# Forget-gate heads: the inverse sums multiply the outputs of the value products instead of the exponentials

## The chip, the cores and the metric

The kernel runs on one core of a Trainium2 chip. The metric is the device time of one execution in microseconds, from the first to the last instruction and the little that lies around them; the median of several runs is quoted. Five engines work side by side: TensorE (PE in the rows, its weight loads PEld), VectorE (DVE), ScalarE (ACT), GpSimd (POOL) and SyncE (SP), which issues most of the DMAs. Each engine takes its own instructions in the order in which the program lists them, and waits on semaphores for the others.

## What is computed

Two blocks of a network follow each other on 256 tokens of width 1024, two layers each: the first block has two gated feed-forward parts, a mixer with several kinds of attention heads, layer norms and a gated projection; the second block has feed-forward parts, a convolution and a windowed attention, and it carries a second sequence of 256 tokens, the context, beside the first. The change concerns the eight forget-gate heads in the mixer of the first block:

```python
def forgetting_attention(q, k, v, f_logit):
    c = jnp.cumsum(jax.nn.log_sigmoid(f_logit.astype(jnp.float32)), axis=1)
    cT = jnp.transpose(c, (0, 2, 1))
    ...
        s = jnp.einsum('bqhd,bkhd->bhqk', qb, k).astype(jnp.float32) * scale + (cq[..., :, None] - cT[..., None, :])
        p = masked_softmax(s, mask)
        return jnp.einsum('bhqk,bkhd->bqhd', p.astype(v.dtype), v)
```

The mixer concatenates their outputs with those of the other heads and multiplies by `w_out`. The mixer runs in both layers.

## The kernel before

Activations lie with the features on the partitions, as tiles of 128 x 8 x 256 (eight chunks of 128 features, 256 tokens). Almost every weight matrix goes through the same path: a DMA brings a tile of 128 x 1024 into a buffer `r`, ScalarE rounds it into a `w` tile (L496), and VectorE subtracts to get the remainder in a second `w` tile (L502). A product is then three matmuls: high weights by high activations, high by low, low by high. That is `mm3`; one weight tile serves 24 matmuls, and up to three tiles are split ahead of their use.

The program is written as Python generators, called streams. The main stream carries the first sequence through all layers. Filler streams carry the context branch of the second block (tiles `f`, `fh`) and the ada product (tiles `a`, products with `csf`, in groups of four matmuls that the trace counts as eight), which the main stream needs only much later. Before anything is built, a planner runs all streams once against a table of costs and writes down which stream goes next at each step; the build then follows that list. When no main instruction is ready on TensorE by the planner's reckoning, it takes filler; when nothing is ready, it puts in single dummy products (`p<-con 128x128`). So any edit in one stream changes the interleaving of all that follows, though the work in each stream stays the same.

In the mixer two workers take jobs from one list, in this order: two `diff` jobs, two `nsa` jobs, four `fox` jobs (0 to 3). A `fox` job serves two forget-gate heads. Each worker holds two buffers of the slots `k` (`R.wk`, four in all): P for the exponentials, T first for the bias row and then for the transposed exponentials. The steps of a fox job are:

- L511: two rows of bias from the cumulative sums into T.
- the scores: 8 products into two PSUM banks for two heads (16 matmuls in the trace), operands `m` and `k,m_ls`.
- `softmax`: VectorE adds the mask and finds the row maximum (L538), ScalarE takes the exponential and sums it (`k<-p,m_qn`), four pieces in all (128 or 256 columns for each head and each half of the queries); VectorE inverts the four sums in one instruction (L544).
- `scaled`: VectorE multiplies each of the four pieces of P by its inverse sum (L509, `k<-k,m_qs`).
- `transposes`: six TensorE transposes of 128 x 128 through the identity matrix `con` (L593), then ScalarE copies four of them into T (128 x 512) and VectorE two (L523).
- `values`: four products of the values with T into a bank O (eight matmuls `p<-k,m` in the trace).
- `finish`: ScalarE rounds O into chunk 4 + j of the mixer's output (`m<-p`), VectorE writes the remainder (`m<-p,m`), and the flag of that chunk is set.

When all eight flags are set, the products with `w_out` begin; each output chunk of 128 reads the eight input chunks 0 to 7 in order, three matmuls each, so that chunk 7 (the last fox job) is first read after 21 matmuls.

Of the kernel before, what the change touches and what calls it, by code (L numbers as in the profile page):

```python
# [14 lines left out]
OP = mybir.AluOpType  # L15
# [461 lines left out]
class Prog:  # L477
# [699 lines left out]
    def mixer(self, l, xs, acc):  # L1177
        R = self.mr
# [10 lines left out]
        for kc in range(8):  # L1189
# [5 lines left out]
            for tb in range(2):  # L1195
                xh = xs[0][:, kc, tb * 128:tb * 128 + 128]
                xl = xs[1][:, kc, tb * 128:tb * 128 + 128]
                for j, (a, b) in enumerate(((0, 512), (512, 916))):
                    o = ps[tb * 2 + j][:, :b - a]
# [65 lines left out]
        o = VEC["fox_b"][0] + l * 8  # L1265
# [20 lines left out]
        def half(i):  # L1286
            return slice(64 * i, 64 * i + 64)
# [111 lines left out]
        def softmax(P, sm, ng, qk, cost=760.0):  # L1399


            pss = []
            for i in range(2):
                pss.append((yield from R.bank((128, 384))))
            group = []
            for qb in range(2):
                ops = [qk(i, slice(qb * 128, qb * 128 + 128), 128 * (qb + 1)) for i in range(2)]
                for k in range(len(ops[0])):
                    group += [(pss[i][:, seg[qb]], *ops[i][k], k == 0, k == len(ops[0]) - 1) for i in range(2)]
            yield from self.mms(group, cost, 128)  # L1410
            for i, ps in enumerate(pss):
                for qb in range(2):
                    self.masked(ps[:, seg[qb]], self.masks[:, 512 - 128 * qb:640], ng[:, i, qb:qb + 1])
                for qb in range(2):
                    self.act(P[:, i, seg[qb]], ps[:, seg[qb]], AF.Exp, scale=-1.0, bias=ng[:, i, qb:qb + 1],
                             accum_out=sm[:, i, qb:qb + 1])
                R.banks.put(ps)
            self.recip(sm, sm)

        def scaled(P, sm):  # L1420
            for i in range(2):
                for qb in range(2):
                    self.ts(P[:, i, seg[qb]], P[:, i, seg[qb]], sm[:, i, qb:qb + 1], None, OP.mult)

        def transposes(P, T):
            ps = yield from R.bank()
            for i in range(2):
                yield from self.tr(ps[:, i, 0:128], P[:, i, 0:128])
                yield from self.tr(ps[:, i, 128:256], P[:, i, 128:256])
            self.act(T[:, :, 0:256], ps)  # L1430
            R.banks.put(ps)
            ps = yield from R.bank((128, 2, 128))
            for i in range(2):
                yield from self.tr(ps[:, i], P[:, i, 256:384])
            self.cp(T[:, :, 256:384], ps)
            R.banks.put(ps)

        def values(T, O, cols, start=True, stop=True):
            o = (O[0:64], O[64:128])
            yield from self.mms([(o[i], V[:, 0, cols(i):cols(i) + 64], T[:, i, 0:256], start, False) for i in range(2)]  # L1440
                                + [(o[i][:, 128:256], V[:, 1, cols(i):cols(i) + 64], T[:, i, 256:384], False, stop)
                                   for i in range(2)], 710.0)

        def finish(src, c):
            OH, OL = out
            self.act(OH[:, c], src)
            self.tt(OL[:, c], src, OH.bitcast(F32)[:, c], OP.subtract)
            self.flags.add(f"{fl_}o{c}")
# [25 lines left out]
        def fox(w, j):  # L1474
            yield from self.until(f"{fl_}fox{j // 2}")
            yield from self.until(fl_ + "pre")
            sm, ng = w.small
            T = yield from self.take(R.wk, (128, 2, 384))
            RT = T[:, 0, 0:256]
            for i in range(2):  # L1480
                b, k = half(i), 2 * j + i
                self.ts(RT[b], cT[b], fm[b, 2 + k:3 + k], fm[b, 10 + k:11 + k], OP.mult, OP.add)

            def qk(i, q, n):
                b = half(i)
                return [(PB[b, j, q], PB[b, 4 + j, :n]), (late[0][b, q], RT[b, :n])]

            P = yield from self.take(R.wk, (128, 2, 384))
            yield from softmax(P, sm, ng, qk, 1420.0)
            scaled(P, sm)  # L1490
            yield from transposes(P, T)
            R.wk.put(P)
            yield from self.until(fl_ + "out")
            O = yield from R.bank((128, 256))
            yield from values(T, O, lambda i: fv + (2 * j + i) * 64)
            R.wk.put(T)
            finish(O, 4 + j)
            R.banks.put(O)

        def diff(w, j):  # L1500
            yield from self.until(fl_ + "diff")
# [44 lines left out]

        out = []
        jobs = [(diff, 0), (diff, 1), (nsa, 0), (nsa, 1), (fox, 0), (fox, 1), (fox, 2), (fox, 3)]

        def worker(w):  # L1550
# [586 lines left out]
```

## Time and profile before

| | us |
|---|---|
| median of 3 runs | 2863.72 |
| lowest and highest of them | 2862.18, 2868.28 |
| the profiled execution, whole | 2864.28 |
| its span, first to last instruction | 2862.5 |
| busy in it: TensorE, weight loads | 2815.1, 2672.2 |
| busy in it: VectorE, ScalarE | 1929.5, 1403.4 |

The mean granted clock of TensorE is 0.992 of full speed. All times in the rows come from the profiled execution. "Busy" of TensorE counts from a matmul's start to its modelled end, and matmuls overlap, so a stretch can be busy and still have lost time between starts; the step from one start to the next is what a matmul takes in a row of them. A step of time in brackets behind a row is the time for which the engine was idle before it, with the one that released it.

### The profile page before, as it was taken

The numbers are of one execution on the slowest core, as the hardware profiler recorded it, in microseconds if no ns is written. First come the engines' busy times: TensorE is split into PE (matmuls) and PEld (weight loads), VectorE is DVE, ScalarE is ACT, GpSimd is POOL, SyncE is SP. The second block draws the span as 40 slices with busy tenths as digits, with TensorE's granted clock in tenths as the row PEclk, the third lists the DMA queues.
The fourth block names the chain that finished last, engine by engine and source line by source line (L and its number), as shares of the span: only waits on it lengthen the run. The fifth ranks groups of instructions, "written<-read, shape, count | busy, mean of one in ns | idle before, by whom it ended". The sixth has DMA issues, their size and how long they took to land.

```text
span 2862.5 us, 55997 instructions
## 1 busy us (share of the span) xinstructions
PE 2815.1 (98%) x23348; PEld 2672.2 (93%) x23348; DVE 1929.5 (67%) x3332; ACT 1403.4 (49%) x2200; POOL 0.2 (0%) x4
## 2 busy tenths in 40 slices
PE   8999999999999999899999999999999999999998
PEld 7999888999999788699899999989999999987998
DVE  4556676656755677899776569998755655576645
ACT  4545544544644554444565454455544554555543
POOL 0000000000000000000000000000000000000000
PEclk9999999999999999999999999999999999999999
DMA  9754554555555664655565555565655565653453
GB/s 342 268 191 164 203 206 170 173 189 188 200 190 186 231 236 141 223 190 183 193 221 184 192 170 198 184 214 166 214 193 184 173 206 186 207 188 134 156 190 113
DMA packets 152846, 553.93 MB, mean 194 GB/s; under 512 B 16272, under 2 KB 26256, under 8 KB 152464
## 3 DMA queue, kind: packets, MB, share of 16 engines
q1 hardware_dynamic: 151728, 548.30, 56.1%
q8 instruction: 183, 3.00, 0.4%
q10 hardware_dynamic: 864, 2.05, 0.2%
q14 instruction: 71, 0.58, 0.1%
HBM read 549.24 MB, written 1.05 MB: 192 GB/s over the span
## 4 chain that ended last, share of the span: by engine, by line
PE 86%; DVE 8%; ACT 3%; DMA 2%; issue 1%; SPq 0%; DVEq 0%; ACTq 0%
PE p L574 84%; DVE w L502 2%; ACT k L496 1%; PE p L593 1%; DVE m L517 1%; DMA a<-ada_w 1%; ACT w L496 1%; DVE f L517 1%; DMA r<-W 1%; DVE m L502 1%; DVE p L538 0%; DVE k L509 0%; ACT m L496 0%; ACT f L496 0%; DVE f L502 0%
## 5 line engine op out<-in xcount | busy, mean ns | idle before, releaser
L574 PE MATMUL p<-m,w 128*128 128x256 f32 x10896 | 1389.7, 282 | 8.7 <-ACT w L496 6.0
L574 PEld LDWEIGHTS p<-m,w 128*128 128x128 f32 x10896 | 1330.0, 189 | 32.9 <-issue 18.1
L502 DVE TENSOR_TENSOR w<-r,w 128x1024 fp32r<-128x1024 f32 (+1 forms) x884 | 1056.2, 1214 | 448.5 <-ACT w L496 438.5
L496 ACT ACTIVATE w<-r 128x1024 fp32r<-128x1024 f32 (+1 forms) x884 | 899.9, 1045 | 438.5 <-PE p L574 289.9
L574 PE MATMUL p<-k,w 128*128 128x256 f32 x4192 | 539.6, 282 | 0.6 <-ACT k L496 0.5
L574 PEld LDWEIGHTS p<-k,w 128*128 128x128 f32 x4192 | 514.0, 188 | 6.8 <-issue 5.6
L574 PE MATMUL p<-f,w 128*128 128x256 f32 x3600 | 492.7, 284 | 1.3 <-ACT k L496 0.9
L574 PEld LDWEIGHTS p<-f,w 128*128 128x128 f32 x3600 | 451.3, 189 | 20.4 <-issue 10.5
L496 ACT ACTIVATE k<-p 128x256 f32<-128x256 f32 (+1 forms) x200 | 80.6, 403 | 354.0 <-PE p L574 351.5
L574 PE MATMUL p<-fh,w 128*128 128x256 f32 x1776 | 252.8, 285 | 0.0
L574 PEld LDWEIGHTS p<-fh,w 128*128 128x128 f32 x1776 | 229.0, 189 | 4.8 <-issue 2.8
L502 DVE TENSOR_TENSOR k<-k,p 128x256 f32<-128x256 f32 x176 | 73.5, 418 | 171.2 <-ACT k L496 170.9
L496 ACT ACTIVATE k<-k 128x256 fp32r<-128x256 f32 (+1 forms) x180 | 74.8, 418 | 123.1 <-DVE k L502 123.1
L502 DVE TENSOR_TENSOR k<-k,k 128x256 fp32r<-128x256 f32 (+1 forms) x176 | 74.8, 425 | 85.2 <-ACT k L496 85.2
L496 ACT ACTIVATE m<-m 128x512 f32<-128x512 f32 (+4 forms) x123 | 64.9, 546 | 92.2 <-DVE m L502 55.7
L517 DVE SCALAR_TENSOR_TENSOR m<-m,vec,m 128x241 f32<-128x241 f32 (+14 forms) x240 | 100.0, 471 | 0.0
L517 DVE SCALAR_TENSOR_TENSOR f<-fh,vec,f 128x241 f32<-128x241 f32 (+14 forms) x240 | 99.2, 470 | 0.0
L574 PE MATMUL p<-a,csf 128*32 128x384 f32 x768 | 86.3, 530 | 3.7 <-DMA a<-ada_w 3.2
L496 ACT ACTIVATE k<-p,m_qn 128x128 f32<-128x128 f32 x96 | 39.0, 419 | 55.5 <-DVE m_qn L538 53.0
L496 ACT ACTIVATE fh<-f_sq 128x256 fp32r<-128x256 f32 x66 | 27.6, 418 | 76.8 <-DVE f_sq L502 61.3
L496 ACT ACTIVATE f_sq<-p 128x256 f32<-128x256 f32 x66 | 24.9, 378 | 71.6 <-PE p L574 71.6
L538 DVE CUSTOM_DVE_ANT_0 p<-p,masksb 128x128 f32<-128x128 f32 (+2 forms) x128 | 55.1, 456 | 4.6 <-PE p L574 3.0
(234 smaller groups left out, 1414.4 us busy)
## 6 DMA issues: line engine op xcount, KB each, us to landing
r<-W SPq DMA_DIRECT2D x876, 512.0 KB, 4.2
a<-ada_w SPq DMA_DIRECT2D x96, 768.0 KB, 4.9
a<-phi_k SPq DMA_DIRECT2D x8, 512.0 KB, 3.5
a<-phi_v SPq DMA_DIRECT2D x8, 512.0 KB, 3.7
m<-xT SPq DMA_DIRECT2D x4, 256.0 KB, 4.2
r<-W SPq DMA_DIRECT2D x8, 128.0 KB, 4.0
f<-ctxT ACTq DMA_DIRECT2D x1, 1024.0 KB, 13.6
out<-m SPq DMA_DIRECT2D x4, 256.0 KB, 2.5
```

The source lines that it names most:

```text
L496: self.nc.scalar.activation(out, in_, func, **kw)
L502: self.nc.vector.tensor_tensor(out=out, in0=a, in1=b, op=op)
L517: self.nc.vector.scalar_tensor_tensor(out, a, s, b, op0=op0, op1=op1)
L538: self.nc.vector.tensor_tensor_reduce(ps, ps, mask, -1.0, 3e38, OP.add, OP.min, ng)
L574: self.nc.tensor.matmul(out, l, r, start=start, stop=stop, skip_group_check=True)
L593: self.nc.tensor.transpose(out, in_, ident[:k, :k])
```

## The change

In a fox job the exponentials in P are no longer multiplied by the inverse sums before they are transposed. Instead VectorE spreads the four inverse sums of the job over a tile of 128 queries x 128 features for each half of the queries (in P's first 256 columns, once the transposes have read them), TensorE transposes the two halves into a PSUM bank `pm`, so that they lie with the features on the partitions as the outputs do, ScalarE copies the output bank O into T, and VectorE multiplies the copy by `pm`. `finish` then reads T in place of O. P, T and one more bank are held until then. The diff and nsa heads keep their scaling.

```diff
             P = yield from self.take(R.wk, (128, 2, 384))
             yield from softmax(P, sm, ng, qk, 1420.0)
-            scaled(P, sm)
             yield from transposes(P, T)
-            R.wk.put(P)
+
+            rb = P[:, 0, 0:256]
+            self.cp(rb.rearrange("p (q a f) -> p q a f", q=2, a=2),
+                    sm.rearrange("p a (q o) -> p q a o", o=1).to_broadcast([128, 2, 2, 64]))
             yield from self.until(fl_ + "out")
             O = yield from R.bank((128, 256))
             yield from values(T, O, lambda i: fv + (2 * j + i) * 64)
-            R.wk.put(T)
-            finish(O, 4 + j)
+            pm = yield from R.bank((128, 256))
+            for qb in range(2):
+                yield from self.tr(pm[:, qb * 128:qb * 128 + 128], P[:, 0, qb * 128:qb * 128 + 128])
+            o = T[:, 0, 0:256]
+            self.act(o, O)
             R.banks.put(O)
+            self.tt(o, o, pm, OP.mult)
+            R.banks.put(pm)
+            R.wk.put(P)
+            finish(o, 4 + j)
+            R.wk.put(T)
```

The planner's list differs from the first mixer on. Over the whole program TensorE gets 16 transposes and 9 dummy products more, VectorE 32 scalings less, 8 copies and 8 products more, ScalarE 8 copies more; everything else is there as often as before.

TensorE at the end of layer 1's mixer, from the transposes of the last two jobs (P in `k_170` and `k_172`) to the first `w_out` product (`m_34`, `w_687`). Before (`a_65` and `a_66` are ada tiles, `f_row` an ada row, `k_169` and `k_171` the jobs' T):

```order
L593 MATMUL p_329_13144<-con,k_170_13089 128x128 x4
L593 MATMUL p_332_13179<-con,k_170_13089 128x128 x2
L593 MATMUL p_331_13173<-con,f_row_13171 128x128 x2
L593 MATMUL p_330_13166<-con,k_172_13114 128x128
L593 MATMUL p_331_13173<-con,f_row_13171 128x128
L593 MATMUL p_330_13166<-con,k_172_13114 128x128
L574 MATMUL p_334_13191<-a_65_13121,csf 32x384 x4
L574 MATMUL p_333_13183<-k_169_13086,m_31_11295 64x256 x2
L574 MATMUL p_333_13183<-k_169_13086,m_31_11295 64x128 x2
L593 MATMUL p_330_13166<-con,k_172_13114 128x128 x2
L593 MATMUL p_335_13212<-con,k_172_13114 128x128 x2
L574 MATMUL p_334_13191<-a_66_13192,csf 32x384 x4
```

and of the changed kernel a piece of the same stretch (`f_6` and `f_7` are the context's activations, `p_336` a bank of its projection, `p_343` the bank `pm` of the first of the two jobs):

```order
L574 MATMUL p_336_13073<-f_6_11156,w_686_12859 128x256
L593 MATMUL p_338_13118<-con,k_172_13054 128x128
L574 MATMUL p_336_13073<-f_6_11156,w_685_12858 128x256
L574 MATMUL p_336_13073<-f_7_11157,w_685_12858 128x256
L574 MATMUL p_336_13073<-f_6_11156,w_686_12859 128x256
L593 MATMUL p_338_13118<-con,k_172_13054 128x128
L593 MATMUL p_341_13174<-con,k_172_13054 128x128 x2
L574 MATMUL p_340_13147<-k_169_13034,m_31_11330 64x256 x2
L574 MATMUL p_340_13147<-k_169_13034,m_31_11330 64x128 x2
L593 MATMUL p_343_13184<-con,k_170_13037 128x128 x2
```

The ada groups have left this stretch, products of the context's projection stand between the transposes (48 of them from the last score block to `w_out`), and two transposes into `pm` follow each job's value products.

ScalarE at the same place, from the last exponential to the first weight split behind the mixer (`m_34` is the rounded output). Before:

```order
L496 ACTIVATE f_row_13171<-p_241_11250 128x384
L496 ACTIVATE k_169_13086<-p_329_13144 128x2x256
L496 ACTIVATE m_34_12432<-p_333_13183 128x256
L496 ACTIVATE k_171_13111<-p_330_13166 128x2x256
L496 ACTIVATE m_34_12432<-p_336_13216 128x256
L496 ACTIVATE w_695_13234<-r_348_13050 128x1024
```

and of the changed kernel:

```order
L496 ACTIVATE k_169_13034<-p_337_13097 128x2x256
L496 ACTIVATE w_693_13151<-r_347_13078 128x1024
L496 ACTIVATE k_171_13051<-p_338_13118 128x2x256
L496 ACTIVATE k_169_13034<-p_340_13147 128x256
L496 ACTIVATE m_34_12362<-k_169_13034 128x256
L496 ACTIVATE f_sq_13203<-p_336_13073,hb_126 128x256
L496 ACTIVATE k_171_13051<-p_342_13179 128x256
L496 ACTIVATE m_34_12362<-k_171_13051 128x256
L496 ACTIVATE w_695_13225<-r_348_13155 128x1024
```

Each job has one evacuation more, from the output bank into T, ahead of the rounding; a weight split and an activation of the context branch stand between them.

## Rows read from the trace of the kernel before

**Rows 1.** The page: TensorE's busy time, and the chain that ended last.
```profile
PE 2815.1 (98%) x23348; PEld 2672.2 (93%) x23348; DVE 1929.5 (67%) x3332; ACT 1403.4 (49%) x2200; POOL 0.2 (0%) x4
...
PE 86%; DVE 8%; ACT 3%; DMA 2%; issue 1%; SPq 0%; DVEq 0%; ACTq 0%
```

**Rows 2.** Busy time by stretches: from:to, length, then the columns named first.
```profile
core 0: us, PE busy (x) PEld busy (x) DVE busy (x) ACT busy (x) POOL busy (x), PEclk, DMA share, GB/s
...
456.00:469.80 13.80, 13.60 (x117) 11.35 (x116) 11.18 (x27) 7.27 (x16) 0.00 (x0) 1.00 0.67 248
1129.10:1147.40 18.30, 17.95 (x157) 14.62 (x156) 14.51 (x45) 8.67 (x26) 0.00 (x0) 1.00 0.29 113
1147.40:1163.30 15.90, 12.11 (x91) 6.54 (x87) 9.28 (x39) 5.28 (x20) 0.00 (x0) 0.79 0.45 149
```

**Rows 3.** Timeline, end of layer 0's mixer: start, length, engine, line, what.
```profile
464.14 4.91 PE L574 MATMUL p<-fh,w 128*128 128x256 f32 x39
...
469.78 9.85 PE L574 MATMUL p<-m,w 128*128 128x256 f32 x81
```

**Rows 4.** Timeline, end of layer 1's mixer.
```profile
1147.43 0.49 PE L574 MATMUL p<-m 64*128 64x128 f32 x4
...
1150.25 0.85 PE L574 MATMUL p<-a,csf 128*32 128x384 f32 x8
...
1152.03 1.01 DVE L509 TENSOR_SCALAR k<-k,m_qs 128x128 f32<-128x128 f32 x4
...
1152.46 1.18 PE L593 MATMUL p<-con,k 128*128 128x128 f32 x6 [1.36 <-DVE k L509]
...
1156.07 0.69 PE L593 MATMUL p<-con,f_row 128*128 128x128 f32 x2 [2.43 <-ACT f_row L496]
...
1163.32 8.85 PEld L574 LDWEIGHTS p<-m,w 128*128 128x128 f32 x75 [0.17 <-issue]
```

**Rows 5.** Timeline: five transposes' loads, a block of value products, an ada group.
```profile
443.52 0.57 PEld L593 LDWEIGHTS p<-con,k 128*128 128x128 f32 x5
...
1145.85 0.87 PE L574 MATMUL p<-k,m 128*64 128x256 f32 x8
...
1146.65 0.16 PEld L574 LDWEIGHTS p<-a,csf 128*32 128x32 f32 x8 [0.17 <-issue]
```

**Rows 6.** Groups by line and shape: count | busy us, mean ns | idle before.
```profile
L496 ACT ACTIVATE w<-r 128x1024 fp32r<-128x1024 f32 x876 | 897.1, 1051 | 438.5 <-PE p L574 289.9 <-DMA r<-W 96.2 <-issue 33.7
...
L502 DVE TENSOR_TENSOR k<-k,p 128x256 f32<-128x256 f32 x176 | 73.5, 418 | 171.2 <-ACT k L496 170.9
...
L496 ACT ACTIVATE k<-p 128x256 f32<-128x256 f32 x176 | 67.0, 381 | 353.6 <-PE p L574 351.5 <-issue 1.7
...
L509 DVE TENSOR_SCALAR k<-k,m_qs 128x256 f32<-128x256 f32 x40 | 13.9, 347 | 0.0
...
L496 ACT ACTIVATE k<-p 128x512 f32<-128x512 f32 x20 | 12.1, 603 | 0.4 <-PE p L593 0.2
...
L509 DVE TENSOR_SCALAR k<-k,m_qs 128x128 f32<-128x128 f32 x40 | 11.3, 283 | 0.7
```

**Rows 7.** The spreading copy of the diff heads: count, ns least/median/most.
```profile
L523 DVE COPY k<-m_nr x4: 293/293/295, 386.6 to 1095.9; 128x256 f32<-128x256 f32 x4
```

**Rows 8.** Timeline of covered jobs: a transpose's wait, and a row of exponentials.
```profile
443.13 0.30 PE L593 MATMUL p<-con,k 128*128 128x128 f32 x1 [0.40 <-DVE k L509]
...
1138.66 0.37 ACT L496 ACTIVATE k<-p,m_qn 128x128 f32<-128x128 f32 x1 [2.14 <-DVE m_qn L538]
...
1139.46 0.37 ACT L496 ACTIVATE k<-p,m_qn 128x128 f32<-128x128 f32 x1
```

**Rows 9.** The chain that ended last, in order of time: start, length, what.
```profile
1153.92 1.72 ACT k L496 x8
```

**Rows 10.** Timeline, the layer norm behind mixer 1.
```profile
1196.80 0.85 PE L574 MATMUL p<-a,csf 128*32 128x384 f32 x8 [1.77 <-DMA a<-ada_w]
...
1198.77 1.05 PE L574 MATMUL p<-con,m 128*128 128x2 f32 x8 [1.11 <-DVE m L517]
```

More of the change, by code (lines that the diff above doesn't have):

```diff
@@ L1495, in fox @@
             yield from values(T, O, lambda i: fv + (2 * j + i) * 64)
+            pm = yield from R.bank((128, 256))
[3 more added lines that the diff above has]
+            self.act(o, O)
+            R.banks.put(O)
+            self.tt(o, o, pm, OP.mult)
+            R.banks.put(pm)
+            R.wk.put(P)
+            finish(o, 4 + j)
             R.wk.put(T)
-            finish(O, 4 + j)
-            R.banks.put(O)
         def diff(w, j):
```

## Prediction

> **What bounds the kernel now.** I read the page first: TensorE is busy for 98% of the span and carries 86% of the chain that ended last [rows 1]. So an instruction taken off another engine is worth only the TensorE time that was lost in waiting for it, and a TensorE instruction that is added costs its own length unless it falls into such a lost stretch. The question is where TensorE loses time near the forget-gate jobs. There are eight of them, four in each mixer; each serves two heads.
>
> The second view is a table by stretches [rows 2]. 456.0:469.8 ends the mixer of layer 0, 1147.4:1163.3 that of layer 1. Both hold the last forget-gate jobs, up to the first product with w_out. In layer 0 the array is busy for 13.60 of 13.8 us at a granted clock of 1.00, in layer 1 for 12.11 of 15.9 us at a mean granted clock of 0.79. The third view, the timeline, says why. In layer 0 the last transposes are followed by 39 products of the filler (the context branch, which runs where the main stream waits) [rows 3]. In layer 1 the filler has run out of ready products before the last two score blocks; from there on only three groups of the ada product stand between main instructions. So TensorE waits 1.36 us for VectorE's scaled exponentials of one job and 2.43 us for a row of ScalarE, and after these pauses part of the stretch runs at the lower clock level, 1.2 GHz [rows 2, 4].
>
> How much is lost there? From the first score product at 1147.43 to the first w_out product at 1163.32 it is 15.9 us [rows 4]. The work in it at full-clock prices: two score blocks, 1147.43 to 1150.25, 2.8 us [rows 4]; 15 transposes at 0.57 / 5 = 0.114 us, 1.7; two blocks of value products at 0.80 (the step from 1145.85 to 1146.65), 1.6; three ada groups at 0.78 (the step from 1146.65 to 1147.43), 2.3 [rows 4, 5]. Sum 8.4, lost 7.5 us. The same account for layer 0, 456.02 to 469.78: one score block 1.4, six transposes 0.7, two value blocks 1.6, one ada group 0.8, and 69 filler products (the last 39 in [rows 3]) at 8.85 / 75 = 0.118 us a product with its weights [rows 4], 8.1. Sum 12.6 of 13.8, lost 1.2. For the covered pair before, 1129.1:1147.4 in layer 1, it leaves 1.6 of 18.3. So a covered pair of jobs loses about 1.4 us, the uncovered one 7.5.
>
> **The change, part by part.** *Removed:* four scalings a job on VectorE, 2 x 0.347 + 2 x 0.283 = 1.26 us [rows 6], 10.1 us in all. They stood between the last exponential and the transposes. TensorE waited for them for up to 0.40 us in a covered job [rows 8] and for 1.36 us in the uncovered one [rows 4]. Off the path they are worth nothing: VectorE is busy for 11.18 of 13.8 us in the covered end [rows 2].
>
> *Added on TensorE:* two transposes a job, 16 x 0.114 = 1.8 us [rows 5], on the engine that sets the end. *Added on VectorE:* a copy that spreads the inverse sums, 0.293 (the like copy in the diff heads) [rows 7], and a product with a PSUM operand, 0.418 [rows 6]; 5.7 us in all, less than what went. *Added on ScalarE:* an evacuation of 0.381 us a job [rows 6], 3.0 us in all, on an engine that is busy for 7.27 of 13.8 us [rows 2]. The evacuation and the product lie one behind the other on the way from the value products to the finished rows: 0.8 us and two handovers. Nobody waits for that in the first seven jobs of a kernel; in the last job of a layer w_out begins with the chunks 0 to 6, 21 x 0.118 = 2.5 us, before it first reads chunk 7. Were that cover gone, it would cost about 0.8 us a layer.
>
> *A new wait on ScalarE:* the rounding of the finished rows waits for VectorE's product, and behind it in ScalarE's order stand the next evacuation and a weight split. It holds them for about 0.4 us and a handover. A split serves 24 matmuls (24 x 0.118 = 2.8 us) and three tiles are split ahead, so I put it at nothing.
>
> *Moved:* the order is planned anew. Both programs hold 5,640 filler products and 384 ada matmuls, so no work is won by it, only idle time. In the new order 48 filler products stand between the last score blocks and w_out of layer 1, where the old one had the three ada groups. Is TensorE then the last there? Its work is 2.8 + 16 x 0.114 + 1.6 + 48 x 0.118 = 11.9 us, plus the 1.4 that a covered pair loses: 13.3. The chain beside it: the second job's exponentials end at 1155.64 [rows 9], 1.0 us sooner when the first job's scalings (1152.03, [rows 4]) no longer stand ahead of its masks, so 1154.6; then two evacuations at 0.603, a weight split at 1.05 [rows 6], value products 0.8, two transposes 0.2 and some handovers, estimated at 1159 to 1159.5, or 12 us after 1147.43. TensorE is the later by a little, so the end is covered. It becomes 2.6 us shorter and holds 5.7 - 2.3 - 0.3 = 3.1 us more filler (0.3 for three transposes of ada rows that left), which is missing elsewhere: 5.7 us, or 6.1 with its four new transposes counted in their own term, the same as 7.5 - 1.4.
>
> The ends of this term are nothing (the pause returns elsewhere, [rows 10]) and 7.5 us (nothing lost at all). I take 6.1, as the covered pairs of both layers agree. Of the other six jobs I expect no gain: most of what they lose is change between shapes, not waiting. Each transpose now waits for its own exponential, where it waited for a scaling; the nearest waits are 0.40 us in a covered job [rows 8] and 1.36 [rows 4], so the difference lies between -0.4 and about 1 us a job. I take 0, since one wait of a kind replaces another, and keep the ends for the range.
>
> The sum: -6.1 + 1.8 = **-4.3 us**. The profiled execution took 2864.28 us (its span of 2862.5 and 1.8 around it), 0.6 above the median 2863.72. So 2860.0 for that execution and 2859.4, say **2859.5**, for the median.
>
> One reading beside this: by busy time the end of layer 1 has 3.8 us free; by weight loads it is loaded for 6.54 of 15.9 us, against 11.35 of 13.8 in layer 0 [rows 2]. The Trainium skill (Perfetto Trace Analysis, Identifying the Most-Contended Engine) holds matmul busy time a poor measure, because matmuls are pipelined, and judges by the share of weight loads. At layer 0's share the stretch would take 6.54 / 0.82 = 8.0 us, 7.9 less, and the kernel 2863.7 - 7.9 + 1.8 = 2857.6, an estimate by that page's rule; by busy time it would be 2861.7. I follow neither; the time by the rule lies in the part of the first rival and moves no chance, since an ada group shows 0.16 us of loads [rows 5] and holds the array for 0.78.
>
> **The rivals.** (1) *More comes back.* The covered jobs, too, lose less, because no transpose waits for VectorE. For it: such waits are in the trace [rows 8]. Price: 0.4 us in six jobs and the whole 7.5 in the tail, -2.4 - 7.5 + 1.8 = -8.1, 2855.6. It counts as faster from -5.7, 2858.0. (2) *The pause only moves.* The filler spent in the tail is missing where TensorE waited next, in the layer norm after mixer 1, which already shows waits of 1.77 and 1.11 us [rows 10]. For it: the convolution taps that the context branch needs next begin later on VectorE. Against: the ada groups pushed out of the tail can fill just such waits. Price: the 16 transposes stay, 2863.7 + 1.8 = 2865.5. (3) *Slower by a new wait.* TensorE takes its row in order, and the transposes now stand behind one exponential each, with three filler products, 0.35 us, between them. If TensorE waits out a job's whole row of exponentials, 1.72 us [rows 9], it loses 8 x 1.72 = 13.8 us and the sum is +9.5, 2873.2; it decides from 1.25 us a job on (8 x 1.25 = 4.3 + 5.7). Against it: the exponentials follow each other at 0.40 us (two in 0.80, [rows 8]), hardly slower than the fillers between.
>
> **How the numbers follow.** A measurement of this kernel can tell 0.2%, 5.7 us, from no change. Chances: forecast, 2858 to 2863, 0.50; rival 1, below 2858, 0.28; rival 2, 2863 to 2869.4, 0.14; rival 3, above, 0.08. So faster 0.28, same 0.64, slower 0.08. The range for 8 in 10 goes from 2855.5 (rival 1 whole) to 2866.5 (rival 2 with 1 us of rival 3).
>
> **What would show it.** Right: in the changed kernel's end of mixer 1 filler stands between the transposes, no TensorE wait there is over 0.5 us, the granted clock is 1.00, and it is about 13.3 us from the second last score block to w_out. Wrong: that stretch is still near 15.9 us; transposes wait over 1 us a job for exponentials; or the layer norm behind it has a pause of several us that was not there.

## The result and the profile after

The changed kernel takes **2882.87 us** (median of 4 runs, 2882.14 to 2885.80); the kernel before took 2864.26 beside it (4 runs). The ratio is 1.0062 with a 95% interval of 1.0050 to 1.0075: slower by 18.6 us. The forecast was 2859.5, its range ended at 2866.5.

The page of the changed kernel, first the busy time, then the chain that ended last by engine, as in [rows 1]:

```profile
PE 2823.5 (98%) x23382; PEld 2682.3 (93%) x23382; DVE 1929.3 (67%) x3316; ACT 1408.2 (49%) x2208; POOL 0.2 (0%) x4
PE 77%; DVE 14%; ACT 4%; DMA 2%; issue 2%; SPq 0%; DVEq 0%; ACTq 0%
```

TensorE is still busy for 98%, but it carries 77% of the chain in place of 86%, and VectorE 14% in place of 8%. So TensorE waits longer, and above all for VectorE. The busy share hides it: the span is 17.8 us longer and the busy time 8.4, because matmuls at half clock, and the 34 records of them that were added, are busy too.

The place on which the forecast rested did what was forecast. The end of mixer 1, from the second last score block to `w_out`, in a table by stretches (columns as in [rows 2]):

```profile
1155.40:1169.00 13.60, 13.04 (x114) 10.82 (x113) 9.51 (x32) 8.05 (x26) 0.00 (x0) 1.00 0.17 53
```

The same stretch in the timeline of TensorE, as [rows 4] show it of before:

```profile
1155.39 0.49 PE L574 MATMUL p<-m 64*128 64x128 f32 x4
...
1158.96 1.33 PE L574 MATMUL p<-f,w 128*128 128x256 f32 x9
1160.71 0.33 PE L593 MATMUL p<-con,k 128*128 128x128 f32 x1 [0.42 <-ACT k L496]
1160.80 0.60 PE L574 MATMUL p<-f,w 128*128 128x256 f32 x3
1161.24 0.27 PE L593 MATMUL p<-con,k 128*128 128x128 f32 x1
...
1167.98 0.87 PE L574 MATMUL p<-k,m 128*64 128x256 f32 x8
1168.78 0.44 PE L593 MATMUL p<-con,k 128*128 128x128 f32 x2
1168.98 1.19 PE L574 MATMUL p<-m,w 128*128 128x256 f32 x8
```

Filler stands between the transposes, the longest wait is 0.42 us, the granted clock is 1.00, and the stretch has become 13.6 us (forecast 13.3; before 15.9, at 0.79 of the clock).

The loss lies elsewhere. The two programs were laid over each other by the 10,896 matmuls `p<-m,w` of the main stream, which stand in the same sequence in both. The table gives, for five stretches of the main stream (times of the kernel before) in one profiled execution of each kernel, what the steps from one matmul to the next hold above the usual step of their kind: as pauses (a step over 0.3 us too long) and as half clock (the other steps in stretches with a granted clock of 0.5).

| stretch, us | pauses before, after | half clock before, after | longer by |
|---|---|---|---|
| up to the layer norm ahead of mixer 1, 0 to 959 | 18.9, 21.8 | 3.7, 2.2 | 2.0 |
| that layer norm and mixer 1, 959 to 1163 | 18.6, 20.8 | 1.9, 5.4 | 3.6 |
| layer norm behind it, to 1229 | 8.0, 8.2 | 0.6, 2.2 | 2.2 |
| convolution, 1381 to 1506 | 7.6, 9.9 | 3.7, 6.8 | 7.9 |
| the rest | 21.5, 21.6 | 1.8, 1.3 | 2.1 |
| sum | 74.6, 82.3 | 11.7, 17.9 | 17.8 |

Of the 17.8 us, 7.7 are pauses, 6.2 half clock and 3.9 all else, the 16 transposes and 9 dummy products that were added among it. How they divide depends on what is taken as the usual step: other choices (by the shape of the matmul alone, or of the next one) give 2 to 9 us of pauses and 5 to 7 of half clock. The runs bear the half clock out: the mean granted clock is 0.989 to 0.991 in the four runs of the changed kernel, and 0.992 in the mean of 20 runs of the kernel before. ("Longer by" counts filler done earlier or later too. By 1012 us the changed kernel is 3.9 us late, but has 18 filler products more behind it. By the first `w_out` product of layer 1 it has done 3 transposes of ada rows and 24 records of ada products less and is 5.7 us late; at 0.114 and 0.10 us each that is some 8.4 us behind.)

Two of its pauses stand before the last forget-gate jobs. The timeline of VectorE and TensorE at the first, where the rotary embedding waits:

```profile
1035.21 0.70 PE L574 MATMUL p<-m,w 128*128 128x256 f32 x3
1035.45 3.50 DVE L502 TENSOR_TENSOR w<-r,w 128x1024 fp32r<-128x1024 f32 x3
1038.87 0.69 DVE L523 COPY m<-p 128x512 f32<-128x512 f32 x1
1039.61 1.38 PE L574 MATMUL p<-m,con 128*128 128x256 f32 x4 [3.70 <-DVE m L523]
1040.42 4.33 PE L574 MATMUL p<-m,w 128*128 128x256 f32 x21
```

TensorE waits 3.70 us for a copy of 0.69 us, in front of which three weight remainders stand in VectorE's order. Not all of this is new. The kernel before waits 3.14 us near this place, for a memset of VectorE, in its timeline of TensorE:

```profile
1030.64 0.63 PE L574 MATMUL p<-a,m_PTc 128*16 128x256 f32 x8 [3.14 <-DVE p L550]
1031.20 2.74 PE L574 MATMUL p<-m,w 128*128 128x256 f32 x21
```

New are 0.6 us of waiting and the 21 products behind it, which take 4.33 us in place of 2.74. The second pause is new as a whole: from 1080 to 1130 us the kernel before has no wait over 0.23 us. In the timeline of all three engines there, one weight remainder stands ahead of the masks of an `nsa` job, and the masks ahead of the exponentials:

```profile
1112.57 1.23 DVE L502 TENSOR_TENSOR w<-r,w 128x1024 fp32r<-128x1024 f32 x1 [0.52 <-ACT w L496]
1113.07 0.44 PE L593 MATMUL p<-con,k 128*128 128x128 f32 x2 [0.47 <-ACT m_PTc L496]
1113.72 0.29 DVE L538 CUSTOM_DVE_ANT_0 p<-p,masksb 128x128 f32<-128x128 f32 x1
1114.69 0.37 ACT L496 ACTIVATE k<-p,m_qn 128x128 f32<-128x128 f32 x1 [1.67 <-DVE m_qn L538]
1115.65 2.29 PE L574 MATMUL p<-f,w 128*128 128x256 f32 x9 [2.14 <-ACT k L496]
```

Behind it TensorE works at the lower level, 1.2 GHz, and so it does in the convolution (where the kernel before has two such stretches of 6.8 us). The two longest in the table by stretches:

```profile
1115.60:1125.80 10.20, 10.15 (x44) 7.55 (x46) 5.33 (x12) 4.58 (x11) 0.00 (x0) 0.51 0.44 177
1419.40:1429.60 10.20, 10.20 (x51) 8.68 (x50) 6.22 (x17) 6.99 (x14) 0.00 (x0) 0.51 0.46 155
```

None of this is in a forget-gate job. So two theories stand against each other. **Theory 1:** the planner's new order costs the time; the new job itself costs its transposes and little more. **Theory 2** (rival 3 of the prediction, widened): the job's own new instructions and waits cost it.

### The profile page after: what moved, and what is told of

Same layout as the page of the kernel before. It is cut to its first block, busy times and chain, and to the rows that moved or that the text cites. A ratio compares the mean times of both kernels' runs of the same rounds, so it can differ in the third digit from the quotient of the medians.

```text
span 2880.3 us, 56086 instructions
## 1 busy us (share of the span) xinstructions
PE 2823.5 (98%) x23382; PEld 2682.3 (93%) x23382; DVE 1929.3 (67%) x3316; ACT 1408.2 (49%) x2208; POOL 0.2 (0%) x4
## 4 chain that ended last, share of the span: by engine, by line
PE 77%; DVE 14%; ACT 4%; DMA 2%; issue 2%; SPq 0%; DVEq 0%; ACTq 0%
PE p L574 76%; DVE w L502 5%; DVE f L517 3%; DVE m L517 2%; ACT k L496 2%; PE p L593 1%; DMA r<-W 1%; ACT w L496 1%; DMA a<-ada_w 1%; DVE m L502 1%; DVE k L502 1%; DVE p L538 1%; ACT f L496 0%; ACT m L496 0%; ACT f_sq L496 0%
## 5 line engine op out<-in xcount | busy, mean ns | idle before, releaser
L502 DVE TENSOR_TENSOR k<-k,k 128x256 fp32r<-128x256 f32 (+1 forms) x176 | 74.8, 425 | 85.2 <-ACT k L496 85.2
```

The source lines that it names most:

```text
L502: self.nc.vector.tensor_tensor(out=out, in0=a, in1=b, op=op)
```

## Experiments: job and order apart

The planner and the build run the same generators, so the planner can be shown one job while the build emits the other into the same steps. That gives the two missing corners of a square.

**New job in the old order.** `pm` is the second half of O's bank, so that no step is added. Against the changed kernel the edit is in pieces:

```diff
+            if self.planning:
+                scaled(P, sm)
+                yield from transposes(P, T)
...
+            else:
...
-            O = yield from R.bank((128, 256))
+                OB = yield from R.bank()
+                O, pm = OB[:, 0], OB[:, 1]
...
-            pm = yield from R.bank((128, 256))
...
-                yield from self.tr(pm[:, qb * 128:qb * 128 + 128], P[:, 0, qb * 128:qb * 128 + 128])
+                    self.nc.tensor.transpose(pm[:, qb * 128:qb * 128 + 128], P[:, 0, qb * 128:qb * 128 + 128], self.con_("ident"))
```

> The planner is shown the old fox job, the build puts the new one into the same places: every filler product, ada group and dummy product stands where it stood in the kernel before, and each job's two transposes into pm follow its value products directly. Theory 1 (the new order of the filler costs the time, the new job itself only its 16 transposes and short waits, 0.95 us a layer as mixer 0 of the changed kernel showed): 2864.3 + 1.9 = about 2866 us; the stretch from 1083 to 1229 us no longer than before by more than 1 us, the one from 1380 to 1506 the same as before. Theory 2 (the new job's own instructions and waits cost it, above all in mixer 1): about 2880 us, with mixer 1 longer by 7 to 8 us. It decides between them at 2873.

Measured: ratio 1.0017 (1.0008 to 1.0026), 4.9 us over the kernel before. **Old job in the new order** is the converse: the planner sees the new job, the build emits the scaled exponentials and leaves the two steps of the transposes empty.

```diff
+            if self.planning:
...
+            else:
+                scaled(P, sm)
...
+                pm = yield from R.bank((128, 256))
+                for qb in range(2):
+                    yield 0.0
+                finish(O, 4 + j)
```

> The converse: the planner is shown the new job, the build emits the old one (scaled exponentials, no transposes into pm, no evacuation ahead of the product) with the filler where the changed kernel has it. Theory 1: the pauses before the forget-gate jobs of mixer 1 and in the convolution stretch stay, so 2882.9 - 1.9 = about 2881 us. Theory 2: about 2864 us, as before. It decides between them at 2873.

Measured: ratio 1.0076 (1.0064 to 1.0089), 21.8 us over the kernel before.

| | old order | new order |
|---|---|---|
| old job | 1 | 1.0076 |
| new job | 1.0017 | 1.0062 |

With either job the new order costs 13 to 22 us. The job costs 4.9 us in the old order (2.3 to 7.5), more than the 1.9 that theory 1 gave it, though far from the 16 of theory 2; in the new order it looks 4 us cheaper than the old one, but there the intervals overlap. Theory 2 falls. The traces show the same: the old job in the new order has the pause of the changed kernel at its place, with the same three remainders ahead of the same copy,

```profile
1036.78 3.50 DVE L502 TENSOR_TENSOR w<-r,w 128x1024 fp32r<-128x1024 f32 x3
1040.19 0.68 DVE L523 COPY m<-p 128x512 f32<-128x512 f32 x1
1040.93 2.07 PE L574 MATMUL p<-m,con 128*128 128x256 f32 x4 [4.53 <-DVE m L523]
```

and the new job in the old order has the pauses of the kernel before in its end of mixer 1 [rows 4], though nothing is scaled there any more (the transposes of the inverse sums are those of L1511):

```profile
1150.38 0.49 PE L574 MATMUL p<-m 64*128 64x128 f32 x4
...
1155.50 1.26 PE L593 MATMUL p<-con,k 128*128 128x128 f32 x6
1159.39 0.69 PE L593 MATMUL p<-con,f_row 128*128 128x128 f32 x2 [2.63 <-ACT f_row L496]
...
1166.98 0.44 PE L1511 MATMUL p<-con,k 128*128 128x128 f32 x2
1167.17 1.06 PE L574 MATMUL p<-m,w 128*128 128x256 f32 x7
```

Its stretch is 16.8 us (1150.38 to 1167.17), no shorter than the 15.9 of before. So the 2.3 us won in the end of mixer 1 were won by filler placed there, not by the scalings that left.

**The new job in one layer alone**, planned as such; for layer 0 the edit is

```diff
+            if l == 0:
+                yield from transposes(P, T)
...
+            else:
+                scaled(P, sm)
...
```

and for layer 1 the same with `if l == 1:`.

> The new job in layer 0 alone, planned as such; layer 1 keeps the old job. Theory 1 in its simple form (the loss in mixer 1 comes from planning the new job there): 2864.3 + 0.95 = about 2865 us. If it is the filler that layer 0 displaces (21 products fewer are done by its w_out) that is missing in mixer 1, then the pauses of 3.98 us at 1035 and 2.4 us at 1113 of the changed kernel are here too and it takes 2872 us or more. Theory 2: half of the loss, about 2873 us.

> The new job in layer 1 alone; layer 0 and all that is planned up to mixer 1 are those of the kernel before. Theory 1 in its simple form: all of the loss but layer 0's part, about 2881 us. If the displaced filler of layer 0 starts it, then 2864.3 + 0.95 = about 2865 us or a little less. Theory 2: about 2873 us.

Measured: 1.0056 (1.0043 to 1.0068), 16 us, for layer 0 alone; 1.0023 (1.0014 to 1.0032), 6.6 us, for layer 1 alone. The simple form of theory 1 falls: most of the loss comes with the edit in layer 0, though nothing is edited behind that layer. In the timeline of TensorE of the kernel with layer 0 alone both pauses of above stand in mixer 1, at the same instructions, where that kernel runs the old job:

```profile
1035.92 1.64 PE L574 MATMUL p<-m,con 128*128 128x256 f32 x4 [2.96 <-DVE m L523]
...
1111.99 2.29 PE L574 MATMUL p<-f,w 128*128 128x256 f32 x9 [2.14 <-ACT k L496]
```

The first is no longer than the 3.14 us of the kernel before, and the loss is not that of the changed kernel over again. Laid over the kernel before by the same products, the profiled execution with layer 0 alone is 6.3 us late at 2500 us and 13.2 at 2619 (its span is 13.2 us longer); the changed kernel goes from 16.2 to 16.6 there. So about half of its loss arises in the second block, far behind any forget-gate job.

Nor is it filler missing after layer 0: it is 21 products behind at `w_out` of layer 0, but at 544 us and still at 900 both programs have done the same filler and ada products, product for product, and go apart only after that. What carries over is then the planner's reckoning of its clocks and of the filler's credit; that is concluded from the counts, no run took it apart.

## Experiments: is it this order, or any other?

**The kernel before with one number of the planner changed**, and no instruction of the streams added, removed or altered:

```diff
-FILLS = (0.25, 0.35, 0.025, 0.0, 0.01, 0.126, 0.056, 0.05, 0, 0.11, 0.35, 1.12, 0.08, 0.25, 0.05, 0.07, 0, 0.1)
+FILLS = (0.25, 0.35, 0.026, 0.0, 0.01, 0.126, 0.056, 0.05, 0, 0.11, 0.35, 1.12, 0.08, 0.25, 0.05, 0.07, 0, 0.1)
```

The third share is that of the mixer of layer 0. In the second kernel the seventh, that of the mixer of layer 1, is 0.058 in place of 0.056.

> The kernel before with one number of the planner changed: the share of filler in the mixer of layer 0 is 0.026 in place of 0.025. No instruction is added, removed or altered, only the order of the filler differs from mixer 0 on. Theory 1a (the old order was a chosen one, and nearly any other costs 10 us or more, whatever the job looks like): 2874 us or more against 2866.3. Theory 1b (only the new job makes the planner find a bad order): 2866 us, within 3.

> The same for the mixer of layer 1: 0.058 in place of 0.056, so the order differs from mixer 1 on alone. Theory 1a: slower too, but by less, since only the second half of what can go wrong is drawn anew: 2869 to 2876 us. Theory 1b: 2866 us, within 3.

Measured: 1.0055 (1.0042 to 1.0068), 15.8 us, and 1.0021 (1.0012 to 1.0029), 6.0 us. That is the size of the change in layer 0 and in layer 1 alone, 16 and 6.6, with the job untouched. Both lie where theory 1a put them. Two draws do not show that nearly any order costs so much, and one thing beside the order did differ: the planner put in 19 and 7 of its own dummy products more (38 and 14 records `p<-con`). At 0.23 us each (32 records in 3.73 us, below) they are worth at most 4.4 and 1.6 us. The trace of the first shows two long pauses in mixer 1, behind VectorE and ScalarE:

```profile
1041.26 1.06 PE L574 MATMUL p<-a,m_PTc 128*16 128x256 f32 x8 [3.89 <-DVE p L550]
...
1120.57 2.72 PE L574 MATMUL p<-f,w 128*128 128x256 f32 x11 [4.19 <-ACT k L496]
```

The first stands at the instruction at which the kernel before waits 3.14 us, the second is new. Its pauses sum up to 85.2 us in place of 74.6, by the account of the table above, and here too 7.9 us of the loss arise between 2500 and 2619 us.

**Both kernels with the planner's shares chosen anew**, in the same way for both, by the planner's own reckoning. For the changed kernel:

```diff
+FILLS = (0.25, 0.3704, 0.0261, 0, 0.0059, 0.1393, 0.0447, 0.0514, 0, 0.0679, 0.346, 1.12, 0.08, 0.2578, 0.0769, 0.07, 0.0058, 0.1003)
```

and for the kernel before:

```diff
+FILLS = (0.25, 0.35, 0.0258, 0.0057, 0.0093, 0.1152, 0.0421, 0.0447, 0, 0.0735, 0.35, 1.12, 0.08, 0.25, 0.0574, 0.07, 0, 0.1)
```

> The changed kernel with the planner's 18 shares chosen anew for it (13 of them differ by a few per cent to a quarter, the other code is the same), as those of the kernel before had been chosen for the old job. Theory 1a: the loss of order goes, and what is left is the job's own cost in place, 4.5 us as e1 measured: 2866 to 2871 us on a chip where the kernel before takes 2866. Theory 1b: it stays at 2880 or above.

> The kernel before with its shares chosen anew in the same way and with as many trials. It gives what the old job takes at its best order by the same search, so that the two jobs are compared with both orders chosen for them: 2862 to 2868 us expected by both theories, 1 to 5 us under e7_after_retuned if the new job costs what e1 measured.

Measured: 1.0002 (0.9993 to 1.0011) for the changed kernel, 1.0006 (0.9996 to 1.0016) for the kernel before. (12 shares differ in the changed kernel, one of them up from 0 and the others by 0.3% to 54%, where the expectation says 13 and at most a quarter.) The 18.6 us of the change are gone, by numbers that touch only the order and the planner's own dummy products (9 fewer than in the changed kernel, as many as in the kernel before). The pauses in its profiled execution are 75.1 us and its half clock 11.9, about those of the kernel before. One execution is not the kernel, though: the profiled one of the old job with new shares has the lowest granted clock of its 11 runs (0.990; the others 0.991 to 0.993), and its span is 6.7 us over that of the kernel before, where the ratio is 1.0006. With an order chosen for each, the two jobs cost the same, within about 0.1%.

## Experiments: the clock behind the pauses

If the half clock follows pauses, dummy products in the pauses should save it. A table tells the build before which TensorE instruction how many go in; the order is untouched:

```diff
+        n = BUSY.get(self.issued, 0)
...
+        if n and banks.free:
+            ps, ident = banks.get((128, 128)), self.con_("ident")
+            for _ in range(n):
+                self.nc.tensor.matmul(ps, ident, ident, start=True, stop=True, skip_group_check=True)
+            banks.put(ps)
...
```

> The kernel before, its order untouched, with dummy products (identity by identity, 89 in 15 places) put into the pauses of TensorE over 0.9 us from 300 us on, as many as fit into each pause at 0.23 us a dummy product. Theory 2a (the half-clock stretches follow pauses in which the array is idle; busy with dummies it stays at full clock): of the 11.7 us that the half clock costs in the profiled run of before nearly all comes back, 2866.5 - 10 = about 2856 us. Theory 2b (dummies do not hold the clock, or the pauses themselves are the whole price): 2866.5 us, within 3.

> The changed kernel, its order untouched, with 109 dummy products in 20 pauses in the same way. It tells how much of the loss of the new order is the half clock behind the pauses (17.8 us in its profiled run, 6.1 more than in before) and how much the pauses. Theory 2a: 2884 - 15 = about 2869 us. Theory 2b: 2884 us, within 3.

> The changed kernel with the shares chosen anew (e7_after_retuned) and dummy products in 14 of its pauses. Theory 2a: 2868 - 10 = about 2858 us, a version that is faster than both kernels. Theory 2b: 2868 us, within 3.

(In the changed kernel one of the 20 places found no free bank, so 102 dummies in 19 pauses went in.) Measured against the kernel before: 1.0038 (1.0024 to 1.0052), 1.0141 (1.0127 to 1.0155) and 1.0075 (1.0063 to 1.0088), all three slower than without dummies (1, 1.0062 and 1.0002). Both theories missed, because many of the dummies waited themselves. In the changed kernel at the pause of the rotary embedding:

```profile
1044.28 0.70 PE L577 MATMUL p<-m,w 128*128 128x256 f32 x3
1049.07 6.26 PE L593 MATMUL p<-con 128*128 128x128 f32 x30 [4.09 <-DVE m L525]
```

The bank that they write is free by the program, but the profile names as what they wait for the very copy that TensorE waits for, so they start when the wait is over and their 6.26 us come on top. Where their bank was free they did what was meant. The pause at 320 us in the timeline of TensorE of the kernel before:

```profile
317.73 2.77 PE L574 MATMUL p<-m,w 128*128 128x256 f32 x22
324.30 1.06 PE L574 MATMUL p<-a,m_PTc 128*16 128x256 f32 x8 [3.80 <-DVE p L550]
325.28 4.58 PE L574 MATMUL p<-m,w 128*128 128x256 f32 x21
```

The stretch behind it in the table by stretches of the same kernel (granted clock 0.66):

```profile
324.00:332.00 8.00, 7.70 (x43) 6.33 (x47) 5.55 (x6) 1.06 (x1) 0.00 (x0) 0.66 0.39 135
```

The same place in the timeline of the kernel before with 16 dummies in the pause (32 in the trace):

```profile
317.81 1.94 PE L577 MATMUL p<-m,w 128*128 128x256 f32 x15
319.58 3.73 PE L593 MATMUL p<-con 128*128 128x128 f32 x32
323.95 0.62 PE L577 MATMUL p<-a,m_PTc 128*16 128x256 f32 x8 [0.64 <-DVE p L552]
324.51 2.75 PE L577 MATMUL p<-m,w 128*128 128x256 f32 x21
```

And its stretch in the table (granted clock 1.00):

```profile
324.00:332.00 8.00, 8.00 (x64) 6.61 (x65) 7.73 (x10) 1.06 (x1) 0.00 (x0) 1.00 0.47 159
```

The wait for VectorE ends at the same instruction, but the 21 products behind it take 2.75 us in place of 4.58 and the clock stays at 1.00. That the activity of TensorE itself holds or drops the clock is also what the Trainium skill says (TensorE: Matmul & The Clock Gate, What's actually happening); this pair of rows agrees. **Dummies only where the bank was free**, in the changed kernel with its own shares:

> The changed kernel with the shares chosen anew and 43 dummy products in the eight pauses where e11_retuned_dummies showed that a dummy finds its bank free; the seven places in which the dummies themselves waited for VectorE are left out. Theory 2a: the half clock behind the pauses at 320 and 1397 us goes, worth 1.85 and about 2.5 us by e9_before_dummies at the same two places, 2868 - 4 = about 2864 us against 2867 of the kernel before. Theory 2b: 2868 us, within 3. If the dummies still push something back: 2870 us or more.

Measured: 2864.11 us, 0.9994 (0.9985 to 1.0003) of the kernel before, where it was 1.0002 without the dummies. Half clock fell from 11.9 to 7.1 us in the profiled execution, pauses from 75.1 to 65.0 (a pause filled with dummies no longer counts as one). The clock rose in every run: its mean is 0.995 or 0.996 in all 11, and 0.990 to 0.993 in 15 of the kernel before. It is the fastest form of the changed kernel tried, and no faster than the kernel before beyond the interval.

## Why the prediction was wrong

*The new job's own terms* held, roughly. The 16 transposes, put at 1.8 us, and the rest, put at nothing, came to 4.9 us (2.3 to 7.5) in the old order and to 0.6 us (-2.0 to 3.2) in an order chosen for the job. The cover by the 21 `w_out` products held: in both layers the longest step among the first 38 of them is 0.20 us. Rival 3 named the wrong wait: transposes wait at most 0.42 us for an exponential in the end of mixer 1.

*The end of mixer 1* held as a place: 13.6 us against a forecast of 13.3, with 48 filler products from the second last score block on, and with all the signs that were named as right. The 6.1 us booked for it were not won.

*The step that failed* is the one on which that booking rests: filler is conserved, so only idle time can be won by moving it, and, unsaid, the stretches that were not looked at stay as they are. The first half is true, the second is not. The same filler in another order left TensorE waiting in other places: 7.7 us more pauses and 6.2 us more half clock over the program; mixer 1, the layer norms ahead of it and behind it and the convolution hold 4.7 us more pauses and 8.2 more half clock. The prediction noted that the order differs from mixer 0 on, and then looked at one stretch of it, where by its account the old order lost 7.5 us, and took the moved filler to shorten the other stretches by just its own length. Its wording "what would show it wrong" asked for a pause in the layer norm behind; that stretch grew by 2.2 us only, its two waits are 1.53 and 1.26 us where they were 1.77 and 1.11 [rows 10]:

```profile
1202.62 0.85 PE L574 MATMUL p<-a,csf 128*32 128x384 f32 x8 [1.53 <-DMA a<-ada_w]
1204.73 1.87 PE L574 MATMUL p<-con,m 128*128 128x2 f32 x8 [1.26 <-DVE m L517]
```

*Rival 2* (the pause only moves) was the right kind with the wrong size: it let what moves cost at most what the end of mixer 1 had won, so that nothing but the transposes was left, 2865.5. The one-number edits show the size that it lacked: an order drawn anew cost 6.0 us from mixer 1 on and 15.8 us from mixer 0 on, with the work of the streams untouched. The chance of 0.08 for slower had no case for that.

*The reading by weight loads* does not help either: their share in the end of mixer 1 rose from 6.54 of 15.9 us to 10.82 of 13.6, and the kernel became slower. By the rule of the Trainium skill (Perfetto Trace Analysis, Identifying the Most-Contended Engine) that stretch has less headroom than before, which agrees with its shorter time. The loss was in others.

What stays open: which of the planner's quantities carries the edit of layer 0 over to mixer 1 and to the second block, and how the 4.9 us of the new job in the old order divide. Its profiled span is 9.8 us over that of the kernel before. Beyond the transposes' 1.8 us it is longer at 1012 to 1060 by 2.6 us and at 1450 to 1506 by 3.1, where its instructions are those of the kernel before: in the first by a wait of 4.15 us in place of 3.14 and half clock behind it, in the second by half clock that the profiled execution of before doesn't have there. So some half clock comes and goes with the same order.

## What to carry to other kernels

Where a planner places filler by its own reckoning, an edit of a few instructions redraws the order of all that follows, and the old order is one that was picked; compare the edit inside the old order and after choosing the planner's numbers anew, not the raw result. A forecast for such an edit needs a term for the redrawn order, best priced by an edit that changes the order alone, and a look at every stretch where the order differs. On an in-order engine look at what stands ahead in the queue of the engine waited for: a copy of 0.7 us behind three weight remainders of 1.2 us held TensorE for 3.7 us.

## What was not expected of the hardware

A pause of TensorE can cost more than its length: behind the 3.80 us at 320 us the next 21 products took 4.58 us in place of 2.75, behind the 3.70 us of the rotary embedding 4.33. Not every pause does: behind 3.14 us in the kernel before they took 2.74, behind 4.15 us at the same instruction of the new job in the old order 3.97. Of the 17.8 us by which the changed kernel's profiled span is longer, about 6 are half clock. And a dummy product helps only if its bank has been read: those at the pause of the rotary embedding started 4.09 us late, with the wait that they were to fill, and the kernel with 102 dummies took 2908.5 us.
